# The up projection of a decoder layer's gated MLP: sixteen pairs of weight tiles in seven products instead of ten, with the steps mixed among the plain tiles

## The chip, the cores and the metric

The kernel runs on one core of one Trainium2 chip. The metric is device time in microseconds of one execution. All weights and activations are fp32 and come from the core's HBM; the output goes back there.

## The reference, cut to what matters

One layer of a hybrid decoder, 256 tokens wide, model width 2048. A normed input goes through a combined projection to an mLSTM and a forgetting attention, their outputs through `w_out` and onto the residual; then the MLP, which is where the change lies; then a gate from a per-layer embedding.

```python
SEQ, D_MODEL, D_FF, CONV_WIDTH = 256, 2048, 5632, 3
h   = rms_norm(x, ffn_norm_g)
z   = h @ w_up                       # (256, 2048) @ (2048, 2 * 5632)
a, g = z[:, :5632], z[:, 5632:]
a   = causal_dwconv(a, conv_w, conv_b)   # y[s] = w2*a[s] + w1*a[s-1] + w0*a[s-2] + b, for each column
x   = x + (gelu(a) * g) @ w_down
```

(The lines on the MLP are written out here in the reference's meaning.)

## The kernel before, in words

**Products.** Every matmul works on fp32 data cut in two rounded parts. A weight block of 128 by 1024 is loaded as it is (`raw`), ScalarE casts it to the high part (`hi`, L1001), VectorE takes the rest (`lo` = raw − hi, L1003). Each block of 128x128 of activations times 128x512 of weights then takes three matmuls (`three()`, L1292 to L1294): ah·hi, ah·lo, al·hi.

**Up projection.** The 5632 columns of `a` and those of `g` are cut into eleven groups of 512 columns each (`q`, 0 to 10). For each group the sixteen k-tiles of 128 rows of `w_up` are loaded one after the other, each with 512 columns of `a` and 512 of `g`. The four outputs (two token tiles t, two halves n) are four PSUM banks, called `up`. A plain k-tile is a unit of 12 matmuls. Two neighbouring k-tiles can be done together, "in seven products": sums of the activations' quarter blocks (`S_up`, made once) times sums of the weights' quarter blocks, seven block products instead of eight, 21 matmuls instead of 24. Four of the products (P1, P5, P6, P7) go to banks of their own (`upP`), the others straight into the `up` banks. In the kernel before, k-tiles 0 and 1 of groups 1 to 10 are such a pair, as four steps in a row after the first six plain tiles (`SEVEN_AT`); group 0 has none. The pair is loaded to a space of its own (L1314 to L1316), and its sums of weights are made by VectorE ahead of the steps (L1323 to L1325).

**After a pair.** The banks P1, P6, P7, P5 are added up into `z_up` in SBUF: ScalarE copies P1 (L1355), VectorE adds P6 (L1356), P7 (L1357) and P5 (L1358). After the last of them has been read, the four banks are free for the next group's `up`: the groups take turns on two sets of four banks ("mm" and "aux"). ScalarE scales `z_up` by the tokens' rstd (L1361).

**After a group.** ScalarE moves the four `up` banks to `EZ`, scaled by rstd (`up_rows`, L887). VectorE adds `z_up` (L894) and turns 32x32 squares (L184) into `Y`; 16 DMAs issued by GpSimd then move the squares to their places in `EZ` (`move`, L190), so that columns lie on partitions. Then the convolution (`up_act`): ScalarE copies `a` (L901), takes the last tap with the bias for each 128 columns (L906), VectorE adds the two others (L909, two for each 128 columns); gelu on ScalarE (L915), times g on VectorE (L916), the split of the result in two parts (L140 on ScalarE, L141 on VectorE), and for pairs that the down projection does in seven products the sums of blocks (`left_sums`, L861 to L866), moved to DRAM by GpSimd (L873).

**Order.** Everything is a list of units (`run_units`). Ahead of a unit, loads are issued by SP (L986) as far as `raw` spaces are free, and the hi and lo of up to four units ahead (`PARTS`) are made, so ScalarE and VectorE run ahead of TensorE by that many units. The jobs after a group are hung behind units of the next group. A scheduler fixes each engine's order of instructions when the program is built; on the chip every engine takes them in that order and waits on semaphores.

Of the kernel before, what the change touches and what calls it, by code (L numbers as in the profile page):

```python
# [15 lines left out]
P = 128  # L16
S = 256
# [18 lines left out]
PARTS2 = 2  # L36
# [7 lines left out]
LO_SHIFT = 16  # L44
FRONT = (8, 4, 4)
LOAD_AT, SUMS_AT, SEVEN_AT = 5, 2, 6
# [3 lines left out]
def layer_kernel(  # L50
# [135 lines left out]
    def move(y, c):  # L186

        for a in range(4):
            for b in range(4):
                pool.dma_start(out=c[32 * b : 32 * b + 32, a::4], in_=y[32 * a : 32 * a + 32, :, b])  # L190
# [54 lines left out]
    def run_stream(blocks, pulls, ramp=False):  # L245
# [4 lines left out]
        for i in range(-AHEAD_DMA, nb):  # L250
            j = i + AHEAD_DMA
            if j < nb:
                src, _, _, load = blocks[j][:4]
                if load is not None:
                    load()
                kb, n = src.shape[1], src.shape[2]
                raws[j] = wp.tile([P, BLK], F32, tag="raw", name=f"raw{j}", bufs=RAW)
                nc.sync.dma_start(out=raws[j][:, : kb * n].rearrange("p (k n) -> p k n", k=kb), in_=src)

            ahead = min(AHEAD_SPLIT, 1 + i // 2) if ramp else AHEAD_SPLIT  # L260
            while i >= -1 and split < min(nb, i + ahead + 1):
                j, split = split, split + 1
                src, _, prep, _, *shift = blocks[j]
                shift = shift[0] if shift else 0
# [5 lines left out]
                hi = wp.tile([P, BLK], F32R, tag="hi", name=f"hi{j}", bufs=PARTS)  # L270
                lo = wp.tile([P, BLK + 64], F32R, tag="lo", name=f"lo{j}", bufs=PARTS)
                hi, lo = hi[:, :w], lo[:, shift : shift + w]
# [537 lines left out]
    with tc.tile_pool(name="ffn", bufs=1) as fp:  # L810
# [6 lines left out]
        S_up = fp.tile([P, 4, 256], F32R, tag="u42", name="S_up")  # L817
        spares = {"u32": (4, 2), "u36": (4, 2), "u40": (2, 1)}
        spare_raws = {k: fp.tile([P, n // 2, BLK], F32, tag=k, name=f"{k}r") for k, (n, _) in spares.items()}
# [26 lines left out]
        B_up = xs[:, 0]  # L846
# [11 lines left out]
        def sums_of(u, f, t):  # L858

            (a11, a21), (a12, a22) = ((u[:, j, 0:P], u[:, j, P:S]) for j in range(2))  # L860
            dve.tensor_add(f[:, 0], a21, a22)  # L861
            dve.tensor_sub(f[:, 1], f[:, 0], a11)
            dve.tensor_sub(f[:, 2], a11, a21)
            dve.tensor_sub(f[:, 3], a12, f[:, 1])
            act.copy(t[:, :, 0:P], f)
            dve.tensor_sub(t[:, :, P:256], f, f32(t[:, :, 0:P]))  # L866
# [9 lines left out]
        a_ = Y[:, 0:BLK].rearrange("p (k s) -> p k s", k=4)  # L876
        c_ = Y[:, BLK : 2 * BLK].rearrange("p (k s) -> p k s", k=4)
# [11 lines left out]
        def up_turn(q):  # L889

            y = Y.rearrange("p (t b c) -> p t b c", t=NT, b=4)
            for t in range(NT):
                if q > 0:
                    dve.tensor_add(EZ[:, t], EZ[:, t], xs[:, 1, t * BLK : (t + 1) * BLK])  # L894
                square(y, t, 0, EZ[:, t])
            move(y, Z)

        def up_act(q):

            def first():  # L900
                act.copy(by_run(a_), runs(Z[:, :, 0:128]))  # L901

            def conv(j):
                def f():
                    k = 4 * q + j
                    act.activation(c_[:, j], a_[:, j], AF.Identity, scale=cT[:, 88 + k : 89 + k],  # L906
                                   bias=cT[:, 132 + k : 133 + k])
                    for d in (1, 2):
                        dve.scalar_tensor_tensor(out=c_[:, j, d:S], in0=a_[:, j, 0 : S - d],  # L909
                                                 scalar=cT[:, 88 - 44 * d + k : 89 - 44 * d + k],  # L910
                                                 in1=c_[:, j, d:S], op0=ALU.mult, op1=ALU.add)
                return f

            def last():
                act.activation(c_, c_, AF.Gelu)  # L915
                dve.tensor_mul(by_run(c_), by_run(c_), runs(Z[:, :, 128:256]))  # L916
                n = 4 if q < KF // 4 - 1 else 2
                for j in range(0, 4, n):
                    split_T(uT(4 * q + j, n), c_[:, j : j + n])
                for p_ in (2 * q, 2 * q + 1):  # L920
                    if p_ in SEVEN:
                        left_sums(p_, c_[:, 2 * (p_ - 2 * q) : 2 * (p_ - 2 * q) + 2])
            return [first, *(conv(j) for j in range(4)), last]
# [3 lines left out]
        made, now = [0], [0]  # L927
        room = {"raw": RAW, "v0": 1, "v1": 1, "v2": 1, "v3": 1, "v4": 1}
        until = {"v0": 8, "v1": 8, "v2": 9, "v3": 9, "v4": 10}
        taken, used = deque(), {}  # L930

        def free_raws(j):

            def may(t):
                if t[0] == "v":
                    return 7 <= j < 16 + 18 * until[t]
                return (t not in ("pT", "ring") or j < late["gate"]) and (t not in ("e0", "e1", "ring") or now[0] > late["free"]) and (t[0] != "x" or j < late["x"])

            return sorted((t for t in room if taken.count(t) < room[t] and may(t)), key=lambda t: used.get(t, -1))

        def new_raw(j, name):
            tag = free_raws(j)[0]
            taken.append(tag)
            used[tag] = len(used) and max(used.values()) + 1
            if tag == "ring":
                return ring[:, 0:2].rearrange("p a b -> p (a b)")
            if tag in ("e0", "e1"):
                return EZ[:, int(tag[1])]
            if tag[0] == "v":
                i = int(tag[1])  # L950
                return spare_raws[f"u{32 + 4 * (i // 2)}"][:, i % 2]
            if tag[0] == "x":
                i = int(tag[1])
                return xs[:, i // 2, (i % 2) * BLK : (i % 2 + 1) * BLK]
            if tag == "raw":
                return wp.tile([P, BLK], F32, tag="raw", name=name, bufs=RAW)
            if tag == "late":
                if tag not in late:
                    late[tag] = apool.tile([P, 2, BLK], F32, tag="aT2", name="w2raw", bufs=2)
                    late["n"] = 0  # L960
                late["n"] += 1
                return late[tag][:, late["n"] % 2]
            return fp.tile([P, BLK], F32, tag=tag, name=name, bufs=room[tag])

        def new_parts(j, shift):
            if late:
                i = made[0] % (PARTS + PARTS2)
                made[0] += 1
                if i < PARTS2:
                    return late["hi"][:, i], late["lo"][:, i]  # L970
            hi = wp.tile([P, BLK], F32R, tag="hi", name=f"hi{j}", bufs=PARTS)
            lo = wp.tile([P, BLK + 64], F32R, tag="lo", name=f"lo{j}", bufs=PARTS)
            return hi, lo[:, shift : shift + BLK]

        class Unit:


            def __init__(self, srcs, fn, split=None, frees=1, shift=0):
                self.srcs, self.fn, self.own, self.frees, self.shift = srcs, fn, split, frees, shift

            def load(self, j):
                self.raws = []
                for i, src in enumerate(self.srcs):
                    kb, n = src.shape[1], src.shape[2]
                    raw = new_raw(j, f"raw{j}_{i}")
                    nc.sync.dma_start(out=raw[:, : kb * n].rearrange("p (k n) -> p k n", k=kb), in_=src)  # L986
                    last["load"] = traced()
                    self.raws.append(raw)

            def split(self, j):  # L990
                hi, lo = new_parts(j, self.shift)
                if self.own is not None:
                    self.own(hi, lo)
                    self.parts = hi, lo
                    return
                kb, n = self.srcs[0].shape[1:3]
                part(hi[:, : kb * n], lo[:, : kb * n], self.raws[0][:, : kb * n])
# [461 lines left out]
```

## Time and profile before

| what | value |
| --- | --- |
| median of 3 runs | 1241.48 us (1240.94 to 1242.33) |
| the profiled execution | 1241.07 us, its span 1239.1 us |
| granted TensorE clock | 1.000 |
| TensorE busy | 1232.5 us, 99% of the span |
| TensorE weight loads | 1039.3 us, 84% |
| VectorE busy | 901.0 us, 73% |
| ScalarE busy | 720.9 us, 58% |
| GpSimd busy | 244.2 us, 20% |
| moved by DMA | 276.35 MB, mean 223 GB/s |

The span runs from the first to the last instruction; the 2.0 us that the execution takes beyond it lie before and behind. The up projection's matmuls run from 432.10 us to 904.93 us, the down projection behind them. Shares of busy time are means over stages with different limits.

### The profile page before, as it was taken

The numbers are of one execution on the slowest core, as the hardware profiler recorded it, in microseconds if no ns is written. First come the engines' busy times: TensorE is split into PE (matmuls) and PEld (weight loads), VectorE is DVE, ScalarE is ACT, GpSimd is POOL, SyncE is SP. The second block draws the span as 40 slices with busy tenths as digits, with TensorE's granted clock in tenths as the row PEclk, the third lists the DMA queues.
The fourth block names the chain that finished last, engine by engine and source line by source line (L and its number), as shares of the span: only waits on it lengthen the run. The fifth ranks groups of instructions, "written<-read, shape, count | busy, mean of one in ns | idle before, by whom it ended". The sixth has DMA issues, their size and how long they took to land.

```text
span 1239.1 us, 16191 instructions
## 1 busy us (share of the span) xinstructions
PE 1232.5 (99%) x5638; PEld 1039.3 (84%) x5638; DVE 901.0 (73%) x1125; ACT 720.9 (58%) x1000; POOL 244.2 (20%) x457
## 2 busy tenths in 40 slices
PE   9999999999999999999999999999999999999998
PEld 7999988888888888888888888888888888888887
DVE  5455566665565665888888898888778998998653
ACT  7565455554554454766676576657645555566542
POOL 2001256513304202022202211220220000050000
PEclk9999999999999999999999999999999999999999
DMA  8766877766557797776877777676895996777560
GB/s 242 207 187 185 233 215 220 207 194 177 173 187 223 217 340 219 223 227 217 260 236 212 224 254 243 192 237 193 257 294 171 316 359 204 264 236 251 179 211 34
DMA packets 134370, 276.35 MB, mean 223 GB/s; under 512 B 15065, under 2 KB 30033, under 8 KB 134161
## 3 DMA queue, kind: packets, MB, share of 16 engines
q1 hardware_dynamic: 118864, 249.66, 64.3%
q0 software_dynamic: 15040, 25.50, 7.2%
q8 instruction: 44, 0.72, 0.2%
q14 instruction: 37, 0.30, 0.1%
q10 hardware_dynamic: 385, 0.16, 0.0%
HBM read 247.46 MB, written 8.93 MB: 207 GB/s over the span
## 4 chain that ended last, share of the span: by engine, by line
PE 99%; DMA 0%; SPq 0%; DVE 0%; ACT 0%; issue 0%; DVEq 0%
PE tg L304 13%; PE tg L305 13%; PE tg L306 13%; PE up L1292 12%; PE up L1294 12%; PE up L1293 12%; PE dnP L1054 1%; PE dnP L1055 1%; PE dnP L1053 1%; PE upP L1292 1%; PE upP L1294 1%; PE upP L1293 1%; PE dn(0, 1)_7885 L1055 1%; PE dn(0, 0)_7881 L1054 1%; PE dn(0, 1)_7885 L1054 1%; PE dn(1, 0)_7889 L1054 1%
## 5 line engine op out<-in xcount | busy, mean ns | idle before, releaser
L275 DVE TENSOR_TENSOR lo<-raw,hi 128x1024 fp32r<-128x1024 f32 (+3 forms) x153 | 177.7, 1162 | 154.8 <-ACT hi L273 154.4
L1294 PE MATMUL up<-hi,x2T 128*128 128x512 f32 x644 | 250.7, 389 | 0.0
L1293 PE MATMUL up<-lo,x2T 128*128 128x512 f32 x644 | 250.6, 389 | 0.0
L273 ACT CAST hi<-raw 128x1024 fp32r<-128x1024 f32 (+3 forms) x153 | 153.1, 1001 | 155.3 <-PE tg L306 122.7
L1292 PE MATMUL up<-hi,x2T 128*128 128x512 f32 x644 | 221.3, 389 | 0.0
L305 PE MATMUL tg<-lo,hT 128*128 128x512 f32 (+2 forms) x480 | 181.5, 379 | 0.0
L304 PE MATMUL tg<-hi,hT 128*128 128x512 f32 (+2 forms) x480 | 180.9, 382 | 0.0
L306 PE MATMUL tg<-hi,hT 128*128 128x512 f32 (+2 forms) x480 | 180.3, 377 | 0.0
L1003 DVE TENSOR_TENSOR lo<-raw,hi 128x1024 fp32r<-128x1024 f32 (+1 forms) x118 | 137.2, 1171 | 43.4 <-ACT hi L1001 42.8
L1001 ACT CAST hi<-raw 128x1024 fp32r<-128x1024 f32 (+1 forms) x118 | 118.8, 1014 | 81.6 <-PE up L1294 35.9
L1294 PEld LDWEIGHTS up<-hi,x2T 128*128 128x128 f32 x644 | 120.9, 188 | 25.1
L1293 PEld LDWEIGHTS up<-lo,x2T 128*128 128x128 f32 x644 | 120.9, 188 | 25.0
L1292 PEld LDWEIGHTS up<-hi,x2T 128*128 128x128 f32 x644 | 120.9, 188 | 25.0
L190 POOL DMA_DIRECT2D EZ<-Y x176 | 93.1, 536 | 122.7 <-DVE Y L184 52.1
L306 PEld LDWEIGHTS tg<-hi,hT 128*128 128x128 f32 x480 | 90.1, 188 | 12.5
L305 PEld LDWEIGHTS tg<-lo,hT 128*128 128x128 f32 x480 | 90.2, 188 | 11.7 <-DVE lo L275 0.3
L304 PEld LDWEIGHTS tg<-hi,hT 128*128 128x128 f32 x480 | 89.7, 188 | 11.7
L1001 ACT CAST hi<-xs 128x1024 fp32r<-128x1024 f32 (+1 forms) x43 | 40.8, 952 | 71.1 <-PE up L1294 50.0
L1003 DVE TENSOR_TENSOR lo<-xs,hi 128x1024 fp32r<-128x1024 f32 (+1 forms) x43 | 47.1, 1098 | 34.7 <-ACT hi L1001 34.7
L873 POOL DMA_DIRECT2D sums<-Sp x9 | 5.2, 575 | 272.3 <-DVE Sp L866 272.3
L1003 DVE TENSOR_TENSOR lo<-u36r,hi 128x1024 fp32r<-128x1024 f32 x36 | 43.6, 1215 | 11.8 <-ACT hi L1001 10.3
L1001 ACT CAST w<-raw 128x1024 fp32r<-128x1024 f32 x27 | 28.4, 1053 | 38.3 <-DVE raw L1102 27.1
(695 smaller groups left out, 2351.9 us busy)
## 6 DMA issues: line engine op xcount, KB each, us to landing
raw<-in_w_in_dram SPq DMA_DIRECT2D x71, 512.0 KB, 4.2
raw<-in_w_up_dram SPq DMA_DIRECT2D x68, 512.0 KB, 5.2
raw<-in_w_down_dram SPq DMA_DIRECT2D x43, 512.0 KB, 6.0
u36r<-in_w_up_dram SPq DMA_DIRECT2D x36, 512.0 KB, 5.0
raw<-in_w_in_dram SPq DMA_DIRECT2D x40, 432.0 KB, 3.8
raw<-in_w_out_dram SPq DMA_DIRECT2D x32, 512.0 KB, 4.7
u32r<-in_w_up_dram SPq DMA_DIRECT2D x31, 512.0 KB, 5.2
EZ<-Y POOLq DMA_DIRECT2D x176, 64.0 KB, 4.6
```

The source lines that it names most:

```text
L190: pool.dma_start(out=c[32 * b : 32 * b + 32, a::4], in_=y[32 * a : 32 * a + 32, :, b])
L273: act.copy(hi, raw[:, :w])
L275: dve.tensor_sub(lo, raw[:, :w], f32(hi))
L304: pe.matmul(o, ah, hi[:, i, :], start=first, stop=False)
L305: pe.matmul(o, ah, lo[:, i, :], start=False, stop=False)
L306: pe.matmul(o, al, hi[:, i, :], start=False, stop=last)
L1001: act.copy(hi, raw)
L1003: dve.tensor_sub(lo, raw, f32(hi))
L1054: pe.matmul(o, ah, lo, start=False, stop=False)
L1292: pe.matmul(o, ah, hi, start=start, stop=False)
L1293: pe.matmul(o, ah, lo, start=False, stop=False)
L1294: pe.matmul(o, al, hi, start=False, stop=stop)
```

## The change

In words, and then the core of the diff.

- Which tiles are pairs, and when their steps come, is now written out as a string for each group (`ORDERS`): `p` is a plain tile, `a` a step of the pair of k-tiles 0 and 1, `b` one of the pair 2 and 3. Groups 0, 2, 4, 6, 8 have both pairs, the others one: sixteen pairs. The steps alternate with plain tiles.
- Where a group has two pairs, P1, P5, P6 and P7 of both add up in the same banks, and the chain that adds them up comes after the last step of `b`, near the end of the group. There is a second set of sums of activations (`S_up[1]`).
- The pair's tiles are loaded to common `raw` spaces; the sums of weights are four additions of 512 columns made in place (L1360, L1361, L1371, L1372), in place of one of 1024 and two of 512.
- The hi and lo spaces have names of their own, and a pair's first step takes one of them instead of two. Spaces are given out by a list (`spaces`), with other rules for the spare ones.
- `z_up` is not scaled by ScalarE: VectorE's addition to `EZ` is an instruction that scales and adds (L895).
- Taps: ScalarE scales all three taps (12 instructions of 256 columns for a group), and VectorE adds two whole tiles of 4x255 and 4x254 (L921). The copy of `a` is gone.
- Of the 16 DMAs that move the squares, ten are issued by SP, behind the last load issued so far, and six by GpSimd.
- In a plain unit the loop over t is now the outer one.

```diff
-PARTS2 = 2
+AHEAD_UP, AHEAD_LATE = 4, 6
...
-LOAD_AT, SUMS_AT, SEVEN_AT = 5, 2, 6
+SEVENS_UP = 2
+ORDERS = ("pppppp" "apapapap" "bpbbbp",
+          *("pppppp" "apapapap" "pppp", "ppp" "apapapap" "bpbpbpb" "pp") * 4,
+          *("pppppp" "apapapap" "pppp",) * 2)
...
-    def move(y, c):
+    def move(y, c, other=None):
         for a in range(4):
             for b in range(4):
-                pool.dma_start(...)
+                (other if other and (4 * a + b) % 3 else pool).dma_start(...)
...
+            def summed(t):
+                return lambda: dve.scalar_tensor_tensor(
+                    out=EZ[:, t], in0=xs[:, 1, t * BLK : (t + 1) * BLK], scalar=rstd2[:, t : t + 1], in1=EZ[:, t],
+                    op0=ALU.mult, op1=ALU.add)
...
+                        with tc.issue_after(last["load"]):
+                            move(y, Z, nc.sync)
...
-                    for d in (1, 2):
-                        dve.scalar_tensor_tensor(out=c_[:, j, d:S], in0=a_[:, j, 0 : S - d], ...)
+                    for d in (1, 2):
+                        act.activation(by_run(taps[d - 1])[:, j], a, AF.Copy, scale=...)
+            def shifted(d):
+                return lambda: dve.tensor_add(c_[:, :, d:S], taps[d - 1][:, :, 0 : S - d], c_[:, :, d:S])
...
+                def sum_of(i, a, hi, lo):
+                    if i not in pb:
+                        pb[i] = bank("mm" if q % 2 else "aux", f"upP{i}")
+                    three(pb[i], *a, hi, lo, r == 0, r == n7 - 1)
...
+                def split3(hi, lo):
+                    ra, rb_ = one.raws
+                    dve.tensor_add(half(ra, 0), half(ra, 1), half(ra, 0))
+                    dve.tensor_add(half(ra, 1), half(rb_, 1), half(ra, 1))
+                    part(hi, lo, ra)
...
+                    if r < n7 - 1:
+                        return
                     z_ = z_up
                     act.copy(z_[:, 0], pb[1])
                     dve.tensor_add(z_[:, 1], pb[6], z_[:, 0])
                     dve.tensor_add(z_[:, 2], pb[7], z_[:, 1])
-                    dve.tensor_add(z_[:, 1::2], pb[5].unsqueeze(1).broadcast_to([P, 2, 512]), z_[:, 1:3])
-                    for t in range(NT):
-                        r = rstd2[:, t : t + 1]
-                        act.activation(z_[:, 2 * t : 2 * t + 2], z_[:, 2 * t : 2 * t + 2], AF.Copy, scale=r)
+                    dve.tensor_sub(z_[:, 1::2], pb[5].unsqueeze(1).broadcast_to([P, 2, 512]), z_[:, 1:3])
```

VectorE, group 2, the chain that adds up P6 (first `upP` row), P7 and P5 (last `upP` row). Names that begin with `lo` (before) or `part_1` (after) are low parts of weight blocks. Before:

```order
L1003 TENSOR_TENSOR lo_4817<-raw_0_4581,hi_4816 128x1024
L1356 TENSOR_TENSOR xs<-upP_4836,xs 128x512
L1003 TENSOR_TENSOR lo_4831<-raw_0_4605,hi_4830 128x1024
L1357 TENSOR_TENSOR xs<-upP_4826,xs 128x512
L1003 TENSOR_TENSOR lo_4844<-raw_0_4626,hi_4843 128x1024
L1358 TENSOR_TENSOR xs<-upP_4822,xs 128x2x512
```

The same chain after:

```order
L1383 TENSOR_TENSOR xs<-upP_4875,xs 128x512
L1032 TENSOR_TENSOR part_1_4983<-raw_0_4828,part_0_4982 128x1024
L927 TENSOR_TENSOR xs<-xs,EZ 128x1024
L1384 TENSOR_TENSOR xs<-upP_4851,xs 128x512
L1032 TENSOR_TENSOR part_1_5020<-u32r,part_0_5019 128x1024
L863 TENSOR_TENSOR Sf<-xs 128x2x128
L1032 TENSOR_TENSOR part_1_5045<-raw_0_4908,part_0_5044 128x1024
L1385 TENSOR_TENSOR xs<-upP_4847,xs 128x2x512
```

Before, the chain stood in the middle of the group with two low parts inside it; after, it stands at the group's end, with three low parts, the product with g (L927) and a sum of blocks (L863) inside it.

TensorE, the border of groups 2 and 3, after: `up_5074` to `up_5077` are the four banks of group 3, `up_5075` the one that P5 of group 2 had; `part_0` is a high part.

```order
L1319 MATMUL up_5075<-part_0_5002,x2T_3577 128x512
L1320 MATMUL up_5075<-part_1_5003,x2T_3577 128x512
L1321 MATMUL up_5075<-part_0_5002,x2T_3577 128x512
L1319 MATMUL up_5075<-part_0_5019,x2T_3577 128x512
L1320 MATMUL up_5074<-part_1_5020,x2T_3577 128x512
```

Between the last matmul of group 2's P6 and the first of these rows stand 31 matmuls. Before, in the middle of a group, P6's last matmul (on `upP_4836`) was followed by more than a hundred of the same group before the next group's first:

```order
L1292 MATMUL upP_4836<-hi_4792,S_up 128x512
L1292 MATMUL up_4708<-hi_4792,x2T_3577 128x512
L1293 MATMUL upP_4836<-lo_4793,S_up 128x512
L1294 MATMUL upP_4836<-hi_4792,S_up 128x512
L1293 MATMUL up_4708<-lo_4793,x2T_3577 128x512
```

SP, the loads at the border of two groups. Before it issues loads alone, the pair's own three (to `xs`) among them:

```order
L986 DMA u36r<-in_w_up_dram 128x2x512 x2
L1314 DMA xs<-in_w_up_dram 128x2x512
L1315 DMA xs<-in_w_up_dram 128x512
L1316 DMA xs<-in_w_up_dram 128x512
L986 DMA u40r<-in_w_up_dram 128x2x512
```

After, ten of the squares' DMAs stand among them:

```order
L1007 DMA u32r<-in_w_up_dram 128x2x512
L1007 DMA raw_0_5048<-in_w_up_dram 128x2x512
L1007 DMA raw_0_5072<-in_w_up_dram 128x2x512
L195 DMA EZ<-Y 32x2x256 x10
L1007 DMA xs<-in_w_up_dram 128x2x512
L1007 DMA u36r<-in_w_up_dram 128x2x512 x2
```

The three loads of the pair's own space are gone; the squares' DMAs stand between the load of a plain block and that of a block for the spare space in `xs`.

More of the change, by code (lines that the diff above doesn't have):

```diff
@@ L922, in last @@
                         left_sums(p_, c_[:, 2 * (p_ - 2 * q) : 2 * (p_ - 2 * q) + 2])
[L923 removed]
+            return [*(scaled(j) for j in range(4)), shifted(1), shifted(2), gelu, gated, parts_of, left]
         late = {}
[L927 to L932, printed above, removed]
[L934 to L939 removed]
```

328 lines of the change are left out of this document (167 added, 161 removed).

## The prediction

> **What bounds the kernel now.** I read the page first, then the waits of TensorE, then busy time by windows, then the timeline of one border between groups. The page's busy row and its chain say that one engine sets the end:
>
> ```profile
> span 1239.1 us, 16191 instructions
> PE 1232.5 (99%) x5638; PEld 1039.3 (84%) x5638; DVE 901.0 (73%) x1125; ACT 720.9 (58%) x1000; POOL 244.2 (20%) x457
> ...
> PE 99%; DMA 0%; SPq 0%; DVE 0%; ACT 0%; issue 0%; DVEq 0%
> ```
>
> TensorE's own waits, in all of the execution, are two, both at the start:
>
> ```profile
> PE warm L93 <- DVE ones L89: 1.1, 1, 1.1
> PE xT L152 <- DMA xs<-in_x_dram: 1.0, 1, 1.0
> ```
>
> So no low part, bank or load comes late today. How near the others are is read by windows (PE, PEld, DVE, ACT, POOL busy, clock, DMA share, GB/s), all of the up projection and one of the down projection:
>
> ```profile
> 430.00:900.00 470.00, 470.00 (x2079) 389.21 (x2079) 383.80 (x449) 301.50 (x356) 89.89 (x169) 1.00 0.75 235
> ...
> 960.00:1000.00 40.00, 40.00 (x178) 33.13 (x177) 39.40 (x46) 23.90 (x27) 0.00 (x0) 1.00 0.93 323
> ```
>
> In the up projection VectorE is busy 383.80 of 470 us (82%), the mean of ten groups with a pair and one without. The second row shows it at 98% for 40 us while TensorE has no gap: a VectorE that is nearly full does not by itself stop TensorE. The price of one product comes from the first and the last of them:
>
> ```profile
> 432.10 0.39 PE L1292 MATMUL up<-hi,x2T 128*128 128x512 f32 x1
> ...
> 904.93 0.39 PE L1053 MATMUL dn(0, 0)_7881<-hi,uA 128*128 128x512 f32 x1
> ```
>
> Between these two starts lie the 2082 products of the up projection before (192 in group 0, 189 in each other group): 472.83 / 2082 = 0.2271 us each. The 0.39 is the length of a pipelined one, and not its price.
>
> **What the change removes.** A pair takes 21 products in place of 24, and six pairs more are 18 products fewer, all on the engine that sets the end: 18 x 0.2271 = 4.09 us. The profiled execution would be 1241.07 - 4.09 = 1236.98, the median 1241.48 - 4.09 = 1237.39. [...]
>
> **VectorE's load.** Its prices are the distances from one start to the next where it does not wait, at one border (VectorE, 691 to 734 us; in brackets what it waited for):
>
> ```profile
> 691.03 2.36 DVE L894 TENSOR_TENSOR EZ<-EZ,xs 128x1024 f32<-128x1024 f32 x2 [0.15 <-ACT EZ L887]
> 693.31 1.23 DVE L184 STREAM_TRANSPOSE Y<-EZ 128x1024 f32<-128x1024 f32 x1
> 694.47 1.18 DVE L1003 TENSOR_TENSOR lo<-u36r,hi 128x1024 fp32r<-128x1024 f32 x1
> ...
> 700.71 0.68 DVE L1003 TENSOR_TENSOR lo<-xs,hi 128x512 fp32r<-128x512 f32 x1
> 701.31 0.68 DVE L1324 TENSOR_TENSOR xs<-xs 128x512 f32<-128x512 f32 x1
> ...
> 708.38 1.23 DVE L1003 TENSOR_TENSOR lo<-xs,hi 128x1024 fp32r<-128x1024 f32 x1 [1.20 <-ACT hi L1001]
> ...
> 719.79 1.23 DVE L1003 TENSOR_TENSOR lo<-u36r,hi 128x1024 fp32r<-128x1024 f32 x1 [2.19 <-ACT hi L1001]
> 720.93 1.27 DVE L909 SCALAR_TENSOR_TENSOR Y<-Y,cT 128x255 f32<-128x255 f32 x3
> 722.12 1.22 DVE L1003 TENSOR_TENSOR lo<-u36r,hi 128x1024 fp32r<-128x1024 f32 x1
> ...
> 730.56 0.29 DVE L861 TENSOR_TENSOR Sf<-Y 128x128 f32<-128x128 f32 x1
> 730.76 0.28 DVE L863 TENSOR_TENSOR Sf<-Y 128x128 f32<-128x128 f32 x1
> ...
> 733.87 1.23 DVE L894 TENSOR_TENSOR EZ<-EZ,xs 128x1024 f32<-128x1024 f32 x1 [0.15 <-ACT EZ L887]
> ```
>
> 1024 columns cost 1.14 us (719.79 to 720.93), 512 cost 0.60 (700.71 to 701.31), one tap of 255 costs 0.40 (three from 720.93 to 722.12), 128 cost 0.20 (730.56 to 730.76), a turn 1.16 (693.31 to 694.47). A second pair replaces two plain low parts (2.28) by one of 512 and three of 1024 (4.02) and adds four sums of 512 (2.40): +4.1 us a group. Every group saves eight taps (3.20) and gets two whole additions of about 1020 columns (2.28): -0.9. The first pair's sums stay as they are (1.14 + 2 x 0.60 before, 4 x 0.60 now). A group lasted 42.84 us (691.03 to 733.87) with 82% of it busy, 35.1 us. One with two pairs gets 35.1 + 4.1 - 0.9 = 38.3 of 186 x 0.2271 = 42.2 us (91%); one with one pair 34.2 of 42.9 (80%). The windows row of 98% is the cover: the load fits, cost nothing, as long as it does not come in lumps larger than VectorE's lead.
>
> **Lumps.** Two rows more of the timeline, of ScalarE and of TensorE, show the lead:
>
> ```profile
> 696.41 1.05 ACT L1001 CAST hi<-u40r 128x1024 fp32r<-128x1024 f32 x1 [1.71 <-PE up L1294]
> ...
> 711.35 0.39 PE L1293 MATMUL up<-lo,S_up 128*128 128x512 f32 x1
> ```
>
> It was narrowest at the pair's steps: the low part of 708.38 above is ready at 709.61, and its first product starts at 711.35, 1.74 us later. VectorE's rows with [.. <-ACT hi] wait for ScalarE, and ScalarE's cast waited 1.71 us for TensorE, that is for a free part space: the lead is full there, not scarce. The largest lump before is two additions and a turn, 691.03 to 694.47, 3.44 us. The largest one now, by the order, is at the end of groups 4 and 8: an addition of 128 columns, two scaled additions, one of 512, two turns and the low part: 0.20 + 2.28 + 0.60 + 2.32 + 1.14 = 6.5 us between two neighbouring low parts, of which TensorE uses the earlier one 13 products (2.95 us) before the later. The lead falls by 3.6 us there. The tiles around are plain ones, so four units ahead are about three plain units of 12 x 0.2271 less one cast and one low part, 8.2 + 0.9 - 2.4 = 6 us or so by these prices. I take it as hidden; uncovered, with a lead of 1.74, it costs 1.9 us each time.
>
> **The banks at a border.** This is the wait that the change adds. With two pairs, the chain that empties P6, P7 and P5 comes at the end of the group, and the next group's `up` wants the banks. In groups 2 and 6 VectorE does, by the rows of the order after, from P6's last product: sum 0.60, low part 1.14, product with g 1.14, sum 0.60, low part 1.14, block sum about 0.33 (between the 0.20 of 128 columns and the 0.60 of 512), low part 1.14, last sum 1.14: 7.2 us. TensorE has 31 products before it wants P5's bank, 7.04 us. With about 0.2 for the last product to drain (0.39 less 0.23) it waits 0.4, and up to 0.9 if VectorE reaches the chain half a low part late. What is queued behind that wait is all of TensorE. At groups 4 and 8 the same count gives 6.4 against 8.3 us, at group 0 about 3.7 against 4.04: no wait. I take 0.5 for each of groups 2 and 6, 1.0 together; the bounds are 0 and 0.9 x 5 = 4.5.
>
> **ScalarE and the queues.** ScalarE's rows (mean ns of one):
>
> ```profile
> L906 ACT ACTIVATE Y<-Y,cT 128x256 f32<-128x256 f32 x40 | 23.0, 597 | 0.0
> ...
> L1361 ACT ACTIVATE xs<-xs,rstd_ffn 128x1024 f32<-128x1024 f32 x20 | 21.9, 1142 | 0.0
> ...
> L901 ACT COPY Y<-EZ 128x1024 f32<-128x1024 f32 x10 | 10.3, 1033 | 0.0
> ```
>
> Each group loses two scalings of `z` (2.28) and the copy (1.03) and gets eight more small scalings, at most 8 x 0.6 = 4.8: +1.5 us, and a second pair adds casts of 1536 columns, about 1.6. ScalarE goes from 301.5 of 470 (64%, 27.5 us a group) to at most 73%. None of it lies on the path. The squares:
>
> ```profile
> 699.68 0.54 SPq L986 DMA_DIRECT2D u40r<-in_w_up_dram  x1
> ...
> 697.71 3.70 POOL L190 DMA_DIRECT2D EZ<-Y  x7 [0.59 <-DVE Y L184]
> ...
> raw<-in_w_up_dram SPq DMA_DIRECT2D x68, 512.0 KB, 5.2
> ...
> EZ<-Y POOLq DMA_DIRECT2D x176, 64.0 KB, 4.6
> ```
>
> GpSimd issues one square in 0.53 us (3.70 / 7), SP one load in 0.54. Ten squares on SP cost it at most 5.4 us, and they wait for the turns, some 5 to 11 us into the group; the loads behind them wait as long, and then need 5.2 us. Weights are loaded about a dozen units ahead, and the loads behind the squares are wanted 8 us and more after they are issued, so this is hidden; without that cover it is up to 2.5 us in the last group, where only four spaces are left for loads, two of them held by the pair's steps. I take 0 to 1 and put 0.1 in the sum. Getting the squares in earlier gains nothing, since TensorE does not wait for them.
>
> **Sum.** 1241.07 - 4.09 + 1.0 + 0.1 = 1238.1 for the profiled execution; on the median, 0.4 higher, 1238.5 us.
>
> **The rivals.** About 0.2% (2.5 us) is what a measurement of this kernel can tell from no change.
>
> 1. *All of the 4.09 arrives.* The chain is 0.2 us longer than its cover by this count, so little is needed: VectorE slightly early, or the block sum cheaper. Time 1237.4. For it: no wait of TensorE in the trace. Against: 7.2 against 7.04.
> 2. *The gain is eaten.* The borders of all five groups with two pairs wait 0.5 to 0.9 (2.5 to 4.5 us), since the chain is handled by an engine at 91%, or the last group's loads are late. Time 1237.4 + 1.6 up to + 6.6, thus 1239.0 to 1244, likeliest 1240. Against: in the down projection VectorE at 98% let nothing wait.
> 3. *Slower: lumps in front of a thin lead.* The 6.5 us lump at the borders meets a lead of 1.74 instead of 6, as it was at the pair's steps before: a wait of 1.9. At five such borders 9.3 us, so 1237.4 + 9.3 = 1246.7. It decides the sign from 1.3 us a border (4.09 + 2.5 over five). For it: steps of a pair are short, 3 or 6 products, and now alternate with plain tiles up to the end of the group, so four units ahead are less time. Against: at the largest lumps the units are plain.
> 4. *The change does not do what it says* (a pair more, but no product less): excluded, the order has 18 matmuls fewer.
>
> **How the numbers follow.** My forecast, a loss of 0.5 to 1.6: 0.42. Rival 1: 0.16. Rival 2: 0.29, nearly all of it within 0.2%, that is 1239.0 to 1244. Rival 3: 0.13. So faster 0.58, same 0.29, slower 0.13. The range reaches from rival 1 less 0.6 (the scatter of the runs before) to most of rival 2: 1236.8 to 1243.0; it leaves out rival 3 and little else.
>
> **What would show it.** The up projection's first product to the down projection's first: 472.83 before, 468.7 if all is gained, 469.7 by my sum. TensorE's waits should show the `up` banks waiting for VectorE's last sum, about 0.5 us, twice (groups 2 and 6), and no wait for a low part. VectorE's busy share in a group with two pairs should be about 91%. I am wrong if TensorE waits for low parts near the borders (rival 3), for loads in the last group, or if the waits for banks are found at all five groups (rival 2).

## The result and the profile after

The changed kernel takes 1236.31 us (median of 6 runs, 1236.08 to 1237.67) where the kernel before took 1241.21 (6 runs, 1240.61 to 1242.38): the ratio on record is 0.9963, with a 95% interval of 0.9952 to 0.9973. It is faster by more than the 0.2% that can be told, and by more than was forecast: 1238.5 with a lower end of 1236.8.

The page of the changed kernel, its busy row and its chain:

```profile
span 1234.2 us, 16266 instructions
PE 1227.8 (99%) x5620; PEld 1035.5 (84%) x5620; DVE 925.0 (75%) x1107; ACT 734.5 (60%) x1071; POOL 185.5 (15%) x347
...
PE 99%; DMA 0%; SPq 0%; DVE 0%; ACT 0%; issue 0%; DVEq 0%
```

TensorE's waits (us in total, times, longest) are the same two as before:

```profile
PE warm L98 <- DVE ones L94: 1.1, 1, 1.1
PE xT L157 <- DMA xs<-in_x_dram: 1.1, 1, 1.1
```

No bank, no low part and no load is waited for. The whole up projection, and four groups by themselves (groups 2 to 5; the first and third have two pairs):

```profile
430.00:900.00 470.00, 470.00 (x2079) 389.23 (x2078) 412.50 (x438) 312.38 (x422) 37.17 (x69) 1.00 0.75 235
...
516.70:558.90 42.20, 42.20 (x188) 34.95 (x187) 37.37 (x39) 29.59 (x40) 3.17 (x6) 1.00 0.70 216
558.90:601.90 43.00, 43.00 (x191) 35.59 (x190) 38.41 (x40) 28.42 (x40) 3.75 (x7) 1.00 0.77 242
601.90:644.10 42.20, 42.20 (x188) 34.95 (x187) 39.13 (x44) 30.60 (x43) 3.78 (x7) 1.00 0.75 234
644.10:687.00 42.90, 42.90 (x190) 35.50 (x190) 37.19 (x38) 27.62 (x39) 3.78 (x7) 1.00 0.77 236
```

VectorE is busy 412.50 us where it was 383.80, up to 93% of a group (39.13 of 42.20), and TensorE has no gap in any of them. The first product of the up projection, the first of the down projection and the last matmul:

```profile
431.54 0.39 PE L1319 MATMUL up<-part,x2T 128*128 128x512 f32 x1
...
900.30 0.39 PE L1080 MATMUL dn(0, 0)_7894<-part,uA 128*128 128x512 f32 x1
...
1229.75 0.28 PE L1277 MATMUL tl<-w,x3T 128*128 128x256 f32 x1
```

The last matmul of the kernel before:

```profile
1234.39 0.28 PE L1250 MATMUL tl<-hi,x3T 128*128 128x256 f32 x1
```

The up projection takes 900.30 - 431.54 = 468.76 us, 472.83 before: 4.07 us less, and 468.76 / 2064 is again 0.2271 us a product. From the first product to the last matmul it is 1229.75 - 431.54 = 798.21 against 1234.39 - 432.10 = 802.29. I call this length the *stretch* from here on. Of the 4.99 us between the two profiled executions (1241.07 and 1236.08) the stretch gives 4.08; 0.56 lie before it, where TensorE's instructions are the same in both kernels, and 0.35 behind the last matmul.

### The profile page after: what moved, and what is told of

Same layout as the page of the kernel before. It is cut to its first block, busy times and chain, and to the rows that moved or that the text cites. A ratio compares the mean times of both kernels' runs of the same rounds, so it can differ in the third digit from the quotient of the medians.

```text
span 1234.2 us, 16266 instructions
## 1 busy us (share of the span) xinstructions
PE 1227.8 (99%) x5620; PEld 1035.5 (84%) x5620; DVE 925.0 (75%) x1107; ACT 734.5 (60%) x1071; POOL 185.5 (15%) x347
## 4 chain that ended last, share of the span: by engine, by line
PE 99%; DMA 0%; SPq 0%; DVE 0%; ACT 0%; issue 0%; DVEq 0%
PE tg L308 13%; PE tg L309 13%; PE tg L310 13%; PE up L1320 11%; PE up L1321 11%; PE up L1319 11%; PE dnP L1082 1%; PE upP L1319 1%; PE upP L1321 1%; PE upP L1320 1%; PE dnP L1080 1%; PE dnP L1081 1%; PE dn(0, 1)_7898 L1080 1%; PE dn(0, 0)_7894 L1080 1%; PE dn(1, 0)_7902 L1080 1%; PE dn(0, 1)_7898 L1082 1%
## 5 line engine op out<-in xcount | busy, mean ns | idle before, releaser
L1321 PE MATMUL up<-part,x2T 128*128 128x512 f32 x608 | 236.6, 389 | 0.0
L1320 PE MATMUL up<-part,x2T 128*128 128x512 f32 x608 | 236.5, 389 | 0.0
L1030 ACT CAST part<-raw 128x1024 fp32r<-128x1024 f32 (+1 forms) x147 | 147.1, 1009 | 112.4 <-PE up L1321 34.2
L1032 DVE TENSOR_TENSOR part<-raw,part 128x1024 fp32r<-128x1024 f32 (+1 forms) x141 | 163.2, 1162 | 34.3 <-ACT part L1030 31.7
L1319 PE MATMUL up<-part,x2T 128*128 128x512 f32 x608 | 185.0, 389 | 0.0
L1319 PEld LDWEIGHTS up<-part,x2T 128*128 128x128 f32 x608 | 114.1, 188 | 23.7
L1321 PEld LDWEIGHTS up<-part,x2T 128*128 128x128 f32 x608 | 114.1, 188 | 23.7
L1320 PEld LDWEIGHTS up<-part,x2T 128*128 128x128 f32 x608 | 114.1, 188 | 23.7
L309 PEld LDWEIGHTS tg<-lo,hT 128*128 128x128 f32 x480 | 90.2, 188 | 11.7 <-DVE lo L279 0.3
L195 POOL DMA_DIRECT2D EZ<-Y x66 | 35.1, 539 | 371.7 <-issue 205.1
L1030 ACT CAST part<-u36r 128x1024 fp32r<-128x1024 f32 (+1 forms) x46 | 47.9, 1043 | 33.5 <-PE up L1321 16.2
L1032 DVE TENSOR_TENSOR part<-u36r,part 128x1024 fp32r<-128x1024 f32 (+1 forms) x46 | 55.6, 1208 | 10.0 <-ACT part L1030 5.8
L1032 DVE TENSOR_TENSOR part<-u32r,part 128x1024 fp32r<-128x1024 f32 (+1 forms) x44 | 50.4, 1146 | 12.2 <-ACT part L1030 9.4
L1030 ACT CAST part<-u32r 128x1024 fp32r<-128x1024 f32 (+1 forms) x44 | 43.5, 994 | 21.1 <-PE up L1321 8.9
L310 PE MATMUL tg<-hi,catT 128*128 128x512 f32 x128 | 49.9, 390 | 0.0
```

Source lines behind the costliest of these rows:

```text
L195: (other if other and (4 * a + b) % 3 else pool).dma_start(out=c[32 * b : 32 * b + 32, a::4], in_=y[32 * a : 32 * a + 32, :, b])
L309: pe.matmul(o, ah, lo[:, i, :], start=False, stop=False)
L310: pe.matmul(o, al, hi[:, i, :], start=False, stop=last)
L1030: act.copy(r32(hi), raw)
L1032: dve.tensor_sub(r32(lo), raw, hi)
L1319: pe.matmul(o, ah, hi, start=start, stop=False)
```

## The experiments

All are read by the stretch, which the start does not touch. "Waits" is the stretch less its products at 0.2271 us, with 798.21 for the changed kernel's; it holds the idle time and what slower products cost. All rows are of one profiled execution each.

| kernel | pairs | stretch, us | waits, us | up projection starts at | time, us |
| --- | --- | --- | --- | --- | --- |
| before | 10 | 802.29 | 0 | 432.10 | 1241.07 |
| changed | 16 | 798.21 | 0 | 431.54 | 1236.08 |
| after_again | 16 | 798.21 | 0 | 433.74 | 1238.30 |
| one_pair | 11 | 801.61 | 0 | 435.12 | 1242.87 |
| fixed_banks | 16 | 798.23 | 0 | 431.84 | 1236.44 |
| taps_dve | 16 | 798.21 | 0 | 431.42 | 1235.78 |
| before_sp | 10 | 802.30 | 0 | 431.46 | 1239.76 |
| ahead3 | 16 | 799.77 | 1.6 | 431.48 | 1237.61 |
| pair17 | 17 | 803.61 | 6.1 | 434.32 | 1244.17 |
| all_two | 20 | 807.18 | 11.7 | 435.61 | 1248.93 |
| blocks | 16 | 811.68 | 13.5 | 431.39 | 1249.22 |
| all_two_late | 20 | 810.71 | 15.2 | 431.26 | 1248.12 |
| chain10 | 16 | 815.87 | 17.7 | 431.61 | 1253.70 |
| pool_squares | 16 | 827.32 | 29.1 | 431.93 | 1265.84 |

### What a product is worth, and what the start gives: one_pair, after_again, before_sp

```diff
-ORDERS = ("pppppp" "apapapap" "bpbbbp",
-          *("pppppp" "apapapap" "pppp", "ppp" "apapapap" "bpbpbpb" "pp") * 4,
-          *("pppppp" "apapapap" "pppp",) * 2)
+ORDERS = ("pppppp" "apapapap" "pppp",) * 11
```

> The changed kernel with one pair in each of the eleven groups (11 pairs in place of 16, everything else as changed). Theory A (the gain is products alone, 0.2271 us each, and nothing else of the change matters): 5 x 3 = 15 products more than the changed kernel, so the up projection lasts 468.76 + 3.41 = 472.2 us and the whole 3.4 us more, about 1239.7; one pair more than the kernel before gives 0.68 of the gain. Rival B (the rest of the change, squares on two queues, taps, spaces, is what gave the 0.8 us more than 4.09): the whole stays 1.5 us or more below the kernel before, near 1238.9 or less.

The stretch is 801.61, 3.40 more than the changed kernel's (15 x 0.2271 = 3.41) and 0.68 less than before (3 x 0.2271): products alone, to 0.01 us. The whole time, 1242.87, is above the kernel before all the same, since this execution's up projection began at 435.12.

> The changed kernel once more, unaltered. If the 0.5 us by which its up projection starts earlier than before (431.54 against 432.10, though nothing ahead of it was changed) is chance in the first microseconds, the start lies anywhere between 431.3 and 432.4 in this profile, and the spread of the times is about 1 us in both kernels; if the change causes it, the start is again within 0.1 us of 431.54.

The same program again: the same stretch, the up projection from 433.74, 2.2 us later than in the first profile; 1236.33 us in the median of 4 runs (1235.89 to 1238.30). So the start moves by 2.2 us with no change in the program. TensorE's row behind its first wait for the input, in the timeline of the kernel before:

```profile
7.41 0.66 PE L152 MATMUL xT<-ident,xs 128*128 128x128 f32 x4 [1.05 <-DMA xs<-in_x_dram]
```

in the changed kernel's:

```profile
6.87 0.66 PE L157 MATMUL xT<-ident,xs 128*128 128x128 f32 x4 [1.09 <-DMA xs<-in_x_dram]
```

in that of after_again:

```profile
7.76 1.12 PE L157 MATMUL xT<-ident,xs 128*128 128x128 f32 x4 [2.27 <-DMA xs<-in_x_dram]
```

and of one_pair:

```profile
7.82 1.11 PE L155 MATMUL xT<-ident,xs 128*128 128x128 f32 x4 [1.23 <-DMA xs<-in_x_dram]
```

The first columns of x land at a slightly different moment each time (the wait for them ends at 7.41, 6.87, 7.76 and 7.82 us), and in the last two the four transposes behind the wait take 1.1 us instead of 0.66: TensorE is at a slower clock there and stays so for the next microseconds. The window of these microseconds in after_again, with the granted clock of 0.50 behind the busy times:

```profile
7.38:10.80 3.42, 3.04 (x9) 2.58 (x10) 2.25 (x6) 2.62 (x7) 0.92 (x4) 0.50 1.07 348
```

By the same view pair17 has 0.50 from 7.86 to 11.28 and all_two from 7.45 to 14.27; in one_pair the products of 512 columns stand 0.43 us apart up to 13.4. These four are the profiles whose up projection begins at 433.7 us or later; the other ten begin between 431.26 and 432.10. From the 60th matmul behind the first transpose of x (18.07 us in the kernel before, 17.52 in the changed one, 21.11 in one_pair) all fourteen take 414.0 us to the up projection, so the spread arises before that matmul, in the first 22 us. The slow phases last 3.42 us in after_again and in pair17 and 6.82 us in all_two; what sets these lengths is not shown.

before_sp is the kernel before with the ten squares' DMAs on SP (`move(y, Z, nc.sync)`).

> The kernel before with ten of the 16 squares' DMAs issued by SP, and nothing else changed. TensorE waited for nothing, and the taps come at the group's end there, so both theories of the changed kernel give no gain: up projection 472.83. The squares were not placed behind the last load by a hint here, so loads may stand behind squares that wait: rival, waits for weights of 0.5 us and more in some groups. The start of the up projection is read too: chance gives 431.3 to 435.7, a cause in the change of the up projection's code gives 432.0 or more for this kernel.

Its stretch is 802.30, so within the stretch two queues for the squares give the kernel before nothing and cost it nothing. Its up projection began at 431.46, earlier than the changed kernel's: the code before the change also starts that early.

### Whether banks are waited for: fixed_banks, chain10

```diff
+    fixed_bank = {"up00": 0, "upP1": 0, "up10": 1, "upP5": 1, "up01": 2, "upP7": 2, "up11": 3, "upP6": 3}
     def bank(tag, name):
-        return ps.tile([P, 512], F32, tag=tag, name=name)
+        i = fixed_bank.get(name, bank_turn[tag] % 4)
+        bank_turn[tag] += 1
+        return ps.tile([P, 512], F32, tag=f"{tag}{i}", name=name, bufs=1)
```

> The changed kernel with the PSUM banks tied to the outputs as the prediction had them: the next group's up10 gets P5's bank, up01 P7's, up11 P6's. If a border wait is a matter of which output sits in P5's bank (the prediction's count: wanted 31 products after P6), TensorE waits 0.4 to 0.9 us at the borders of groups 2 and 6, 1 us in all. If the scheduler puts the products in the order in which the banks come free whatever they are called (P5's bank again 50 products after P6 in the order), it waits for nothing: up and down projection, to the last product, 798.2 us as in the changed kernel.

It waits for nothing (798.23), as the second theory had it. In the program's order of this kernel up10 is now the last output to be begun, 50 products after P6, exactly where up11 stands in the changed kernel. In the changed kernel the built program gives group 2's P1, P5, P7, P6 the banks 4, 5, 6, 7 and group 3's up00, up10, up01, up11 the banks 4, 6, 7, 5: P5's bank, the last to come free, goes to up11. So `up_5075` in the order shown ahead of the prediction, which is up10, has P7's bank and not, as the text there says, P5's. The changed kernel's chain on VectorE at that border in the timeline (the sums with P6, P7, P5):

```profile
554.60 0.69 DVE L1383 TENSOR_TENSOR xs<-upP,xs 128x512 f32<-128x512 f32 x1
...
557.48 0.69 DVE L1384 TENSOR_TENSOR xs<-upP,xs 128x512 f32<-128x512 f32 x1
...
560.68 1.22 DVE L1385 TENSOR_TENSOR xs<-upP,xs 128x1024 f32<-128x1024 f32 x1
```

TensorE, from P6's last product:

```profile
554.18 0.39 PE L1321 MATMUL upP<-part,S_up 128*128 128x512 f32 x1
...
561.43 0.39 PE L1319 MATMUL up<-part,x2T 128*128 128x512 f32 x1
...
565.74 0.39 PE L1319 MATMUL up<-part,x2T 128*128 128x512 f32 x1
```

The chain takes 7.3 us (554.60 to 561.90), as counted. By the program's order the product of 561.43 is the first into P7's old bank, 3.3 us after that was read (558.17), and the one of 565.74 the first into P5's, 3.8 us after the chain's end. The trace alone says as much: the product of 561.43, the one behind the 31 counted, starts 0.47 us before the chain has read P5's bank to its end (561.90), so that bank is not the one it writes. Had it been, it would have waited about 0.5, the price in the prediction.

chain10 lengthens the chain: ten more additions that read P7 and write where the last sum writes later, in groups 2 and 6.

```diff
+                    for _ in range(10 if q in (2, 6) else 0):
+                        dve.tensor_add(z_[:, 3], pb[7], z_[:, 2])
                     dve.tensor_sub(z_[:, 1::2], pb[5].unsqueeze(1)...)
```

> The changed kernel with ten additions of 512 columns more (their result is overwritten) in the chain that empties the banks, before its last sum, in groups 2 and 6 alone: the chain there grows from 7.2 to 13.2 us. By the prediction's count (P5's bank is wanted 31 products, 7.04 us, after P6) TensorE would wait about 6 us twice: up projection 468.8 + 12 = 481. Rival (banks are handed out in the order in which they come free, and the bank of P5 goes to the last of the next group's outputs, 50 products or more later): under 1.5 us in all, up projection below 470.3.

Both numbers were wrong: 17.7 us of waits. The scheduler put the ten between other work, seven of them in one piece, so the chain became 17.7 us long (554.66 to 572.35), not 13.2, and P7's bank was held as well:

```profile
566.06 5.04 DVE L1386 TENSOR_TENSOR xs<-upP,xs 128x512 f32<-128x512 f32 x7
571.13 1.22 DVE L1387 TENSOR_TENSOR xs<-upP,xs 128x1024 f32<-128x1024 f32 x1
```

TensorE behind the wait:

```profile
571.15 0.80 PE L1319 MATMUL up<-part,x2T 128*128 128x512 f32 x1 [4.98 <-DVE xs L1386]
...
572.17 0.63 PE L1321 MATMUL up<-part,x2T 128*128 128x512 f32 x1
572.60 0.63 PE L1319 MATMUL up<-part,x2T 128*128 128x512 f32 x1
```

and the window of the same time, with the granted clock behind the busy times:

```profile
571.10:575.00 3.90, 3.85 (x9) 3.11 (x10) 3.83 (x4) 0.00 (x0) 0.00 (x0) 0.50 0.00 0
```

The waiting product starts at 571.15, just after the last addition that reads P7 and while the sum that reads P5 is still at work (571.13 to 572.35): here too the first bank wanted late is P7's. So a bank wait can be had: this chain is 10.4 us longer than the changed kernel's, which left 3.3 and 3.8 us. It is paid for twice here: after it the granted clock is 0.50 (up to 576.44 by the same view), the products are 0.43 us apart (572.17 to 572.60), and the wait of 5.0 us costs 7.7, a second one in group 6 7.3. Shorter waits make up the rest of the 17.7.

### How much cover there is: ahead3, taps_dve

```diff
-AHEAD_UP, AHEAD_LATE = 4, 6
+AHEAD_UP, AHEAD_LATE = 3, 6
```

> The changed kernel with parts made three units ahead instead of four in the up projection. It measures how much lead there is over the lumps. By the prediction's sum the lead is about 6 us and the largest lump takes 3.6 of it: with three units it is about 3.5, so waits of 0 to 0.5 us at the borders of groups 4 and 8 only, up projection below 470. Rival C (the lead is already nearly used up, as the run with 20 pairs suggests): waits at all five borders of groups with two pairs, 1 us and more each, 474 and more.

Waits of 1.6 us, all after 879 us, in the last group; none at a border. So with a quarter of the lead taken away the lumps of the changed kernel are still covered, and the expectation named the wrong place: in the last group casts wait for loads, the one of 879.00 for 3.55 us.

taps_dve puts the two taps back on VectorE, as eight instructions for a group.

> The changed kernel with the taps as in the kernel before: one copy of a by ScalarE in pieces, the last tap on ScalarE, the two others by eight VectorE instructions for a group. VectorE gets 0.9 us more in each group (93% instead of 91% in those with two pairs), ScalarE 1.5 us less. Theory A (only what comes late counts): waits only if the eight instructions make a lump of their own; up projection 468.75 to 470. Rival (the run with 20 pairs and the one with all squares on GpSimd show that the changed kernel stands at an edge): waits of 1 us and more in each of the five groups with two pairs, 474 and more.

The stretch is the same, 798.21. VectorE is busy 419.58 us of the 470 (412.50 in the changed kernel), and nothing waits: where the taps are worked out is worth nothing here.

### What the mixing, the alternation and the queues are worth: blocks, pool_squares, all_two, all_two_late, pair17

```diff
+ORDERS = ("pppppp" "aaaa" "pppp" "bbbb" "pp",
+          *("pppppp" "aaaa" "pppppppp", "ppp" "aaaa" "pppp" "bbbb" "ppppp") * 4,
+          *("pppppp" "aaaa" "pppppppp",) * 2)
```

> The changed kernel, the same 16 pairs, but the four steps of a pair in a row (pppppp aaaa pppp bbbb pp and the like) in place of alternating with plain tiles. Theory A (only products count as long as nothing waits) with the lumps' rule: four steps are 21 products, 4.8 us, in which VectorE has to give three low parts of 1024, one of 512 and four sums, 6.4 us, after about 6 us of lead: no wait in groups with one pair, at most 0.5 us in groups with two, up projection 468.8 to 471. Rival (the mixing is what keeps the gain): waits at the steps of both pairs, 1 us and more for each of 16 pairs, above 480.

13.5 us of waits; the up projection takes 482.2 us, above the rival's 480, with 0.84 us a pair where it said 1 and more. Four steps in a row take parts faster than they are made. TensorE's waits:

```profile
PE upP L1319 <- ACT part L1030: 3.7, 5, 1.0
PE up L1319 <- ACT part L1030: 2.2, 4, 0.7
...
PE up L1320 <- DVE part L1032: 1.0, 2, 0.8
```

They sum to about half of the 13.5. Behind the first cluster the granted clock is 0.50 for 3.4 us (452.74 to 456.15), which costs about 1.9 (nine products take from 452.42 to 456.37). The rest are waits too short for this list, and the first 0.16 us of each one in it, since a product's bar in the profile is 0.39 us long and its spacing 0.227. Mixing steps with plain tiles is what makes sixteen pairs possible at all.

pool_squares leaves all 16 DMAs of the squares to GpSimd: `move(y, Z)` for `move(y, Z, nc.sync)`.

> The changed kernel with all 16 DMAs of the squares issued by GpSimd, as in the kernel before. Theory A (TensorE waits for nothing, so the queue of the squares is worth nothing): up projection 468.75 us, unchanged. Rival Q (squares that arrive 3 to 5 us later make the scaling of the taps on ScalarE late, and the casts queued behind it): waits of TensorE on ScalarE's casts of up to 1 us a group with two pairs, 469.5 to 474.

29.1 us of waits, far beyond both. The first scaling of the taps on ScalarE in group 2, in pool_squares:

```profile
548.14 0.60 ACT L914 ACTIVATE xs<-EZ,cT 128x256 f32<-128x256 f32 x1
```

a product of TensorE's there, a little later:

```profile
557.91 0.50 PE L1320 MATMUL up<-part,x2T 128*128 128x512 f32 x1 [2.26 <-DVE part L1032]
```

and the same scaling in the changed kernel:

```profile
537.20 0.60 ACT L914 ACTIVATE xs<-EZ,cT 128x256 f32<-128x256 f32 x1
```

With one queue the squares are in place later: GpSimd issues the last of them at 541.75 us, after 2.9 us of waits for earlier ones to land, where SP issued it at 534.8, and from issue to landing they take 6.1 us in the median, not 2.3. The scalings stand 10.9 us further back in ScalarE's order, one after the other (548.14 to 553.3, no cast among them). The two additions of taps then fall into the chain at the group's end (554.92 and 557.78 on VectorE), with the low parts behind them, and TensorE waits 2.26 us for one. What is shown so is this wait alone: the stretch has twelve others of 0.2 us and more, 4.7 us of them in the down projection, and the clock is at 0.50 for 17 us in all. In the kernel before, the chain was over in the middle of the group and the taps came after it, so one queue was enough: before_sp gained nothing.

all_two has both pairs in groups 0 to 8 (`*("ppp" "apapapap" "bpbpbpb" "pp",) * 8` for the groups 1 to 8); all_two_late the same with the string of group 0 in all nine.

> The changed kernel with two pairs in each of the groups 0 to 8 (20 pairs, 12 products fewer than the changed kernel). Theory A (VectorE at some 91% in every such group still hides everything): up projection 468.76 - 2.73 = 466.03 us, whole 1233.6. Rival C (VectorE needs the groups with one pair to recover its lead): waits for low parts or banks at the later borders, 0.5 us and more in each of eight groups, so no gain or a loss: 1236 to 1240.

1248.67 us (1248.19 to 1249.21), 11.7 us of waits and 7 us slower than before: a ratio of 1.0053 (1.0038 to 1.0068), slower than either theory gave. Of the profiled execution's loss the stretch is 4.9 us, and the late start gives most of the rest. VectorE in all_two, at a border:

```profile
655.68 0.69 DVE L1032 TENSOR_TENSOR part<-u32r,part 128x512 fp32r<-128x512 f32 x1
656.28 2.49 DVE L895 SCALAR_TENSOR_TENSOR EZ<-xs,rstd_ffn,EZ 128x1024 f32<-128x1024 f32 x2
658.67 0.30 DVE L865 TENSOR_TENSOR Sf<-xs,Sf 128x128 f32<-128x128 f32 x1
658.87 0.70 DVE L1360 TENSOR_TENSOR u32r<-u32r 128x512 f32<-128x512 f32 x1
659.47 2.38 DVE L189 STREAM_TRANSPOSE Y<-EZ 128x1024 f32<-128x1024 f32 x2
661.76 1.20 DVE L1032 TENSOR_TENSOR part<-u36r,part 128x1024 fp32r<-128x1024 f32 x1
```

and TensorE:

```profile
663.01 0.50 PE L1320 MATMUL up<-part,x2T 128*128 128x512 f32 x1 [1.60 <-DVE part L1032]
```

For 5.5 us (656.28 to 661.76) VectorE makes no low part, the next group's first pair steps are near, and TensorE waits until the low part of 661.76 is ready. The longest wait of this run, 3.2 us for a cast of ScalarE at the next border, goes back to a lump of the same kind: that cast (707.58) had waited 2.30 us for a sum of weights that VectorE made at 706.83, behind two turns. This is the prediction's third rival, a lump in front of a thin lead, in another kernel. In the changed one six plain tiles stand at that place after every group with two pairs.

> Two pairs in each of the groups 0 to 8 as in the run with 20 pairs before this, but each group begins with six plain tiles (the string of group 0, pppppp apapapap bpbbbp). In the order VectorE's turn of the group's result then lies among low parts of plain tiles, at most 3.6 us between two low parts in place of 6.3, while the banks are wanted sooner (P5's bank 26 to 32 products, 5.9 to 7.3 us, after P6, against a chain of about 6.3 us). Theory L (the waits of the run with 20 pairs came from lumps on VectorE that meet the next group's early pair steps): up projection 466.0 to 467.5 us, whole 1233.6 to 1235. Rival M (VectorE's mean load of 92% is too much without groups of one pair between): waits of 1 us and more at each border as before, up projection 474 or more. Rival N (banks): waits on the last sum of the chain, about 0.5 us at each of eight borders, 470.

1248.41 us (1248.12 to 1249.22). Smaller lumps did not help: 15.2 us of waits, none of them listed with more than 0.7 us. Rival M holds for this kernel; whether it is the mean load or the spacing of the steps was not separated.

pair17 gives the last group the second pair.

> The changed kernel with two pairs in the last group too (17 pairs; a group of one pair stands ahead of it, as everywhere). Theory A with alternation (a group with two pairs costs nothing behind one with one pair): three products fewer, up projection 468.07 us, whole 0.68 us less than the changed kernel. Rival (the last group has only four spaces for loads, and the run with three units ahead waited just there): waits of 1 to 3 us at its end or at the start of the down projection, up projection 469.5 to 472.

1242.50 us (1241.44 to 1245.01), 6.1 us of waits, all of them after 880 us: the last group has no room for it. Its first wait stands behind a cast of ScalarE (881.00) that waited 5.17 us for a load, and SP issued the loads of that time from 876.27 on, behind ten squares (869.31 to 876.17). No version tried beats the changed kernel; taps_dve equals it.

## Why the prediction was wrong, point by point

- **What a product is worth** was right: 4.09 forecast, 4.08 measured, and 0.68 a pair in one_pair. The up projection took 468.76, where the prediction had 468.7 for the whole gain. (Eight small transposes of x lie among the 2082 products, from 436.18 us on; they make the price of 0.2271 about 0.2% too high.)
- **The step that failed is the banks at a border**, the term of 1.0 us. The chain was sized rightly (7.2 forecast, 7.3 measured), but I took P5's bank to be the one wanted after 31 products. The scheduler hands banks out as they come free and puts the products in that order, so P7's is wanted after 31 and P5's after 50, 3.8 us after it is free; fixed_banks shows that the names do not matter. The wait was 0. The first rival, "all of the 4.09 arrives", was what happened, and it had 0.16.
- **The loads of the last group**, 0.1: nothing either, though ahead3 and pair17, where casts wait for loads, show that this is where the cover is thinnest. Ten squares hold SP for 7.4 us (528.07 to 535.44), not for 5.4 at most.
- **The low end of the range** allowed 0.6 us of scatter below the full gain, and that was too little: without the two terms above the forecast would have been 1237.4, and the median of 1236.31 lies 1.1 below it. Of the 2.0 us between the sum (1238.1) and the profiled execution (1236.08), 1.1 are the two terms; the other 0.9 lie ahead of the stretch (0.56) and behind it (0.35). The start moved between 431.26 and 435.61 in the profiles, and the kernel before was profiled at 432.10, so chance can give this much. That it is chance alone is not shown: the 34 executions of the kernel before on record have a median of 1241.4 us and the ten of the changed one 1236.3, 5.1 apart where the stretch gives 4.1. Of the ten profiles without a slow phase at the start, the two of programs that leave all squares to GpSimd (before and pool_squares) begin the up projection latest, at 432.10 and 431.93, and all others take less than their 2.0 and 2.3 us outside the span (1.7 to 1.9). A part of the queues in this was not separated.
- **The lumps and the lead.** No low part came late, as taken. The sum behind the lead of 6 us (8.2 + 0.9 - 2.4) makes 6.7, and its 0.9 stands in no row; ahead3 shows that three units cover the lumps too.
- **VectorE's load** was roughly right (91% in groups with two pairs; 89 and 93% in the two shown), 80% in the others too low (87 to 89%), since the turn of a big group falls into the next. That it costs nothing there was right, and ahead3 backs it.
- **The squares** were misjudged. "Getting the squares in earlier gains nothing" holds for the kernel before and not for the changed one: with its taps early and its chain late, one queue costs 29.1 us. The way it does so is shown for group 2.

## What to carry to other kernels

Where one engine has no gap, count its instructions: the gain of removing some is their spacing (0.2271 us each here), and it arrives whole (here 4.08 us of 4.09) as long as every other edit only moves work under cover. Before pricing a wait for a buffer, look up which buffer the built program really reuses, and in what order; a scheduler that hands out what came free first hides short chains (here one of 7.3 us). A mean load read from a kernel that waits misleads: in the same 470 us all_two has VectorE no fuller than the changed kernel (415.60 and 412.50), but only since its waits stretch the time. Over the whole up projection its work is 425.3 us, 91% of the 466.0 that its products take, against 411.1 of 468.8 (88%) in the changed kernel and 418.4 (89%) in taps_dve, which waits for nothing. Two of the waits of all_two go back to lumps that meet short steps; whether a load of 91% would have stood there without them is open.

## What the hardware showed that was not expected

In chain10 a wait of TensorE cost half as much again as it lasted: after each of its two waits of 5.0 us the granted clock was 0.50, products stood 0.43 us apart instead of 0.227, and the waits cost 7.7 and 7.3 us. In pool_squares a shorter wait, of 2.26 us, was followed, 0.9 us after its end, by a clock of 0.50 as well (558.79 to 562.20), and in all_two one of 3.17 us was not (1.00 from 700 to 714). So the length of a wait alone does not decide it; what else does was not separated. In the slow phases timed from end to end above, the granted clock stayed at 0.50 for 3.4 us (after_again, pair17, blocks, pool_squares) or 6.8 us (all_two). The first 22 us, the same products in all these programs, decide up to 4.4 us of the time (up projection from 431.26 to 435.61); what differs there in the rows above is when the first columns of x land (6.87 to 7.82 us) and how long the four transposes behind that wait take (0.66 us in the kernel before and the changed one, 1.1 in after_again and one_pair). A comparison to 0.1 us has to be read behind that point.
